# Causal softmax: dividing by the row sums before or behind the product with the values, in a two-layer decoder on one core

## The chip, the cores and the metric

One Trainium2 chip (trn2), one of its cores. The metric is device time in microseconds. Engines: TensorE (PE; its weight loads are shown apart as PEld), VectorE (DVE), ScalarE (ACT), GpSimd (POOL) and SyncE (SP), which issues the DMAs. Each engine works through its own instructions in the order in which they were written out.

## The reference

Two layers of a decoder over 512 tokens of width 1024, all in fp32. Each layer: an RMS norm and one input projection that feeds two branches, a latent attention of eight heads with a causal softmax and a state-space scan; both are normed and go through one output projection; then a cross-attention into 256 memory tokens and a gated feed-forward part. What matters here is the softmax of the eight heads, in query blocks of 128:

```python
s = (einsum(qn[lo:hi], k_nope[:hi]) + einsum(qr[lo:hi], k_rope[:hi])).astype(float32)
s = where(mask, s, -inf)
p = softmax(s, axis=-1)
outs.append(einsum('bhqk,bhkd->bqhd', p, v[:, :, :hi]))
```

## The kernel before, in words

Activations lie feature-major: partitions are features, the free dimension is the 512 tokens. An fp32 product is made of three float32r products, of a high and a low part of each operand (`mm3`, lines 213 to 219: lines 216, 217, 218). `split` (lines 232 to 245) makes the two parts: ScalarE copies the high one (line 238), VectorE or GpSimd subtracts for the low one (line 239).

The attention of a layer is `mla` (line 746). It runs over 16 units, a head `hd` and a half `I` of the queries; a unit holds query blocks 2I and 2I+1. Scores of unit u are issued ahead of the values' product of unit u-1. For each unit:

- `mla_score` (line 693) makes four products a block into PSUM (lines 707 to 710, tag "s", three banks), the rows being queries. `softmax` (line 765) takes the negated maximum on VectorE (767), the exponential with its sum on ScalarE (768), the reciprocal of the sum on VectorE (769), and scales P by it: on VectorE (773), or on ScalarE (771) where `NORM` (line 158) says "a", which is block 3 of layer 0.
- `mla_out` (line 715) transposes P by blocks of 128x128 on TensorE (728) into PSUM banks of tag "t", splits them (lines 238, 239), and multiplies with the values (736 to 738) into a bank of tag "mm". For an even head the weight has 64 columns and the result lies in partitions 0 to 63; for an odd one the weight has 128 columns, and partitions 64 to 127 are used. Behind the second unit of a head the half is copied to `a_out`: on ScalarE for even heads (742), on VectorE for odd ones (744). Two heads share one tile `a_out[pair]` of 128x512.

Tags "t" and "mm" have two banks each (line 146); "t" also serves the row norms (lines 272 to 299) and, in the state-space branch, the gate's products (line 923).

Between the units other work is placed by `PLAN` (line 165): the scan on VectorE (`s5_scan`, line 800, operations at 818 to 822 and 848 to 851), its products on TensorE (792, 877, 892), the gate (927), and the keys and values of the memory for the cross-attention (`xkv`, line 944, evacuated at 959). `OFFS` (line 176) gives each such part a priority, and the scheduler writes out each engine's order from the priorities and from its own simulation of the times (line 1203). `row` (line 272) is the kernel's existing way of laying values of tokens along the free dimension: an fp32 product of a broadcast column with the identity (277).

After the attention, `mix_out` (line 996) norms `a_out` and adds its half of the output projection to the state-space half.

Of the kernel before, what the change touches and what calls it, by code (L numbers as in the profile page):

```python
# [13 lines left out]
AF = mybir.ActivationFunctionType  # L14
ALU = mybir.AluOpType
# [119 lines left out]
class Trunk:  # L135
    def __init__(self, ctx, tc, A, out, depth=L, dbg=None):
# [8 lines left out]
    BUFS = {"raw": 3, "whi": 2, "wlo": 2, "wraw": 2, "hi": 17, "lo": 17, "ghi": 4, "glo": 4, "tmp": 5, "tmps": 3, "R": 4, "s5b": 6, "P": 4,  # L145
            "mm": 2, "f": 1, "s": 3, "t": 2, "sm": 8, "stat": 4, "sc": 3}

    # Which engine forms the low parts and the like (per layer where there are two), and PSUM tags.
    XKV_POOL = tuple(range(16))
# [7 lines left out]
    MN_POOL, MW_POOL = ((1, 3, 5, 7), (0, 2, 4)), ((), ())  # L157
    NORM = ("vvva", "vvvv")
    YT, GT = "f", "t"
    TAIL = 2  # L160
    STOP = 0

    # What runs between the attention units of a layer: (unit, part, index), and how much later than
    # its place in the order each part may run.
    PLAN = ((
# [26 lines left out]
    @contextmanager  # L192
    def later(self, off):
        """Lower the priority of what is emitted inside."""
        self.tc.cur_priority += off
        yield
        self.tc.cur_priority -= off
# [3 lines left out]

# [1 line left out]
    def load_w(self, ap, eng=None):  # L203
# [17 lines left out]
    def after(self, ins, dep):  # L221
        """Keep ins behind dep in the schedule (no wait)."""
        if dep is not None:
            self.tc.add_manual_dep(ins.ins, dep.ins.name,
                                   mybir.DependencyInfo(mybir.DependencyClass.NoSync, mybir.DependencyReason.DATA),
                                   reason="order")
        return ins
# [4 lines left out]
    def split(self, src, scale=None, out=None, lo_eng=None, dep=None):  # L232
        """src (* scale) as the exact sum of two float32r parts."""
        nc = self.nc
        eng = lo_eng or nc.vector
        hi, lo = out or self.slot()
        if scale is None:
            a = nc.scalar.activation(hi, src, AF.Copy)  # L238
            b = eng.tensor_tensor(lo, src, hi.bitcast(F32), ALU.subtract)  # L239
        else:  # L240
            a = nc.scalar.activation(hi, src, AF.Copy, scale=scale)
            b = eng.scalar_tensor_tensor(lo, src, scale, hi.bitcast(F32), ALU.mult, ALU.subtract)  # L242
        self.after(a, dep)
        self.after(b, dep)
        return hi, lo

    def load_w_slots(self, ap):
        """A narrow weight block, kept in operand slots of 512 columns."""
        out = []
        for c in range(0, ap.shape[-1], 512):  # L250
            n = min(512, ap.shape[-1] - c)
            raw = self.t([128, 512], "raw")[:, :n]
            self.nc.sync.dma_start(raw, ap[:, c:c + n])
            out.append(self.split(raw, out=[x[:, :n] for x in self.slot()]))
        return out

    def square(self, acc, x, eng=None, tag="tmp"):
        """Add the squares of x to acc."""
        sq = self.t([128, 512], tag)[:, :x.shape[-1]]
        self.nc.scalar.activation(sq, x, AF.Square)  # L260
        if acc is None:
            return sq
        (eng or self.nc.vector).tensor_tensor(acc, acc, sq, ALU.add)
        return acc
# [7 lines left out]
    def row(self, col):  # L272
        """Values of tokens down the partitions, laid along the free dimension of every partition."""
        nb = col.shape[-1]
        ps = self.p("t")[:, :nb * 128]
        for b in range(nb):
            self.nc.tensor.matmul(ps[:, b * 128:(b + 1) * 128], col[:, b:b + 1].to_broadcast([128, 128]), self.ident,
                                  start=True, stop=True)
        return ps

    def rms(self, acc, dim):
        """1/rms per token, as a column and along the free dimension."""
        nc = self.nc
        acc = acc if isinstance(acc, list) else [acc]
        n = acc[0].shape[-1]
        nb = n // 128
        ps = self.p("t")
        for b in range(nb):
            for i, x in enumerate(acc):
                nc.tensor.matmul(ps[:, b:b + 1], x[:, b * 128:(b + 1) * 128], self.ones, start=i == 0,  # L290
                                 stop=i == len(acc) - 1)
        ms = self.t([128, 4], "stat")[:, :nb]
        nc.vector.tensor_scalar(ms, ps[:, :nb], 1.0 / dim, EPS, ALU.mult, ALU.add)
        col = self.t([128, 4], "stat")[:, :nb]
        nc.gpsimd.tensor_tensor(col, ms, self.mhalf[:, :nb], ALU.pow)
        ps2 = self.row(col)
        R = self.t([128, 512], "R")[:, :n]
        nc.scalar.activation(R, ps2, AF.Copy)
        return col, R

# [1 line left out]
    def setup(self):  # L302
# [93 lines left out]

# [1 line left out]
    def load_pk(self, l):  # L398
# [165 lines left out]

# [1 line left out]
    def normed(self, l, name):  # L566
# [14 lines left out]
    def mm_block(self, ap, X, ps, m=128, eng=None):  # L581
        """One output tile [m, 512] of W^T X."""
        hi, lo = self.pre.pop(0) if self.pre else self.load_w(ap, eng)
        self.mm3(ps, [((hi[:, k * m:(k + 1) * m], lo[:, k * m:(k + 1) * m]), X[k]) for k in range(len(X))])
# [82 lines left out]
    def mla_qk(self, l, hd):  # L667
        """Key and query operands of one head: rows [nope | rope | swapped rope], or rope first for odd heads."""
        nc = self.nc
# [22 lines left out]

    def mla_score(self, qk, I):
        """Softmax rows of query blocks 2I and 2I+1."""
        nc = self.nc
# [4 lines left out]
        else:  # L700
            sc = [(self.p("s")[:, :384], self.t([128, 512], "P")[:, :384]), (self.p("s"), self.t([128, 512], "P"))]
        st = self.t([128, 8], "sm")
        for ii, (ps, p) in enumerate(sc):
# [7 lines left out]
        for ii, (ps, p) in enumerate(sc):  # L711
            self.softmax(ps, p, st[:, 4 * ii:4 * ii + 4], self.NORM[self.l][2 * I + ii])
        return [p for _, p in sc]

    def mla_out(self, hd, I, p, po):
        nc = self.nc
# [22 lines left out]
        if I == 1:  # L739
            a = a_out[pair]  # L740
            if par == 0:
                nc.scalar.activation(a[0:64], po[0:64], AF.Copy)
            else:
                nc.vector.tensor_copy(a[64:128], po[64:128])

    def mla(self, l, hooks):
# [4 lines left out]
        for u in range(2 * H + 1):  # L751
            if u < 2 * H:
                hd, I = u // 2, u % 2
                pend.append((hd, I, self.mla_score(qk[hd], I)))
            if u >= 1:
                out = pend.pop(0)
                if out[1] == 0:
                    po = self.p("mm")
                self.mla_out(*out, po)
            if u < 2 * H and I == 0 and 0 < hd < H - 1:  # L760
                qk[hd + 1] = self.mla_qk(l, hd + 1)
            for f, a in hooks.get(u, ()):
                f(*a)

    def softmax(self, ps, p, st, eng):
        nc = self.nc
        nc.vector.tensor_reduce(st[:, 0:1], ps, mybir.AxisListType.X, ALU.max, negate=True)
        nc.scalar.activation(p, ps, AF.Exp, bias=st[:, 0:1], accum_out=st[:, 1:2])
        nc.vector.reciprocal(st[:, 2:3], st[:, 1:2])
        if eng == "a":  # L770
            nc.scalar.activation(p, p, AF.Copy, scale=st[:, 2:3])
        else:
            (nc.gpsimd if eng == "p" else nc.vector).tensor_scalar(p, p, st[:, 2:3], None, ALU.mult)

# [25 lines left out]
    def s5_scan(self, l, piece):  # L800
# [9 lines left out]
        def step(dst, src, k, nj):  # L810
            """dst += A^k src (complex, over [128, 2, 16, nj])"""
            t1 = self.t([128, 2, 16, 8], "sc")[:, :, :, :nj]
# [51 lines left out]
    def s5_y0(self, q):  # L864
        """The part of y that no state carries."""
        nc = self.nc
# [77 lines left out]
    def xkv(self, l, X, ms):  # L944
        """Key (first half) and value columns of the memory, both feature-major."""
        nc = self.nc
# [31 lines left out]
    def mix_s(self, l):  # L978
        """The state-space half of the output projection's operands."""
        self.load_h(self.A["xT"] if l == 0 else self.dh)  # L980
# [3 lines left out]
    def mix_w(self, l, m, tag):  # L984
        """The state-space half of one output tile."""
        ps = self.p(tag) if tag else self.pm()
# [220 lines left out]
```

## Time and profile before

| | |
|---|---|
| median of 3 runs | 1632.43 us |
| the runs | 1628.01, 1632.43, 1634.59 us |
| span of the profiled execution | 1624.2 us (first to last instruction; its own time is not listed beside it) |
| mean granted TensorE clock | 0.966 of full |
| busy: PE, DVE, ACT, POOL | 1517.3, 975.1, 619.6, 345.8 us |

Spans are those of one profiled execution; start and end of a run lie around them. "Busy" leaves out waits, branches and DMA issues. The granted clock is the share of full speed that TensorE's throttle let through: 1.0 is 2.4 GHz, 0.5 is 1.2 GHz. Starts are counted from the span's first instruction.

### The profile page before, as it was taken

Reading aid. Unit: us, or ns where it says so; the run is one execution under the profiler, and the core shown is the slowest. Engines: PE = TensorE matmul, PEld = TensorE weight load, DVE = VectorE, ACT = ScalarE, POOL = GpSimd, SP = SyncE. Lnnn points to the kernel's source line nnn. Section 1 sums busy time; section 2 is a strip of 40 time slices with the busy share of each in tenths; the row PEclk is TensorE's granted clock in tenths of the full one; section 3 lists DMA queues with packets and bytes.
Section 4 is the critical chain, followed back from the end, with each engine's and each line's share of the span. In section 5 each row is a group of like instructions: output and inputs, shape, how many; then the busy total and the mean of one; then the engine's idle time right before and its main releaser. Section 6 shows DMA issues by size and latency. Waiting matters only on the chain.

```text
span 1624.2 us, 20486 instructions
## 1 busy us (share of the span) xinstructions
PE 1517.3 (93%) x8038; PEld 1272.5 (78%) x8038; DVE 975.1 (60%) x1499; ACT 619.6 (38%) x995; POOL 345.8 (21%) x225
## 2 busy tenths in 40 slices
PE   7779798999999999999998778989999999999997
PEld 6558687788778888888886777878888888888886
DVE  6985966866764434435453996685555443443554
ACT  5344357444333313223242534753443331322333
POOL 4553443402421100101100354430000110010110
PEclk9879799999999999999999989999999999999998
DMA  6174444321443232232248515332212222223222
GB/s 224 62 130 105 85 138 135 105 91 42 127 136 99 103 96 99 89 106 91 88 156 155 133 42 146 124 118 93 75 41 92 93 102 99 96 91 105 91 90 75
DMA packets 97488, 169.09 MB, mean 104 GB/s; under 512 B 32496, under 2 KB 55536, under 8 KB 97392
## 3 DMA queue, kind: packets, MB, share of 16 engines
q1 hardware_dynamic: 97392, 167.79, 34.7%
q8 instruction: 63, 1.03, 0.3%
q14 instruction: 33, 0.27, 0.1%
HBM read 150.00 MB, written 15.66 MB: 102 GB/s over the span
## 4 chain that ended last, share of the span: by engine, by line
PE 67%; DVE 9%; ACT 4%; DMA 2%; issue 2%; POOL 1%; SPq 1%; DVEq 0%; ACTq 0%; POOLq 0%
PE mm L216 13%; PE mm L218 13%; PE mm L217 12%; PE f L216 7%; PE f L217 7%; PE f L218 7%; ACT whi L209 1%; DVE lo L239 1%; ACT hi L238 1%; DVE s5b L927 1%; DVE wlo L210 1%; DVE sc L818 1%; PE mm L1006 1%; PE mm L1005 1%; DMA s5b<-du 1%
## 5 line engine op out<-in xcount | busy, mean ns | idle before, releaser
L209 ACT ACTIVATE whi<-wraw 128x1024 fp32r<-128x1024 f32 (+1 forms) x234 | 243.3, 1042 | 637.1 <-PE mm L217 312.3
L210 DVE TENSOR_TENSOR wlo<-wraw,whi 128x1024 fp32r<-128x1024 f32 (+2 forms) x196 | 279.4, 1426 | 68.1 <-ACT whi L209 65.9
L216 PE MATMUL mm<-hi,whi 128*128 128x512 f32 x589 | 231.3, 393 | 0.3 <-ACT whi L209 0.3
L218 PE MATMUL mm<-hi,wlo 128*128 128x512 f32 x589 | 230.0, 392 | 0.4 <-DVE wlo L210 0.4
L217 PE MATMUL mm<-lo,whi 128*128 128x512 f32 x589 | 229.7, 391 | 0.0
L1113 POOL TENSOR_TENSOR tmp<-tmp,tmp 128x512 f32<-128x512 f32 x44 | 60.4, 1374 | 573.8 <-DVE tmp L1112 518.9
L216 PE MATMUL mm<-ghi,whi 128*128 128x512 f32 (+1 forms) x368 | 147.1, 400 | 9.3 <-ACT whi L209 7.9
L218 PE MATMUL mm<-ghi,wlo 128*128 128x512 f32 (+1 forms) x368 | 146.5, 398 | 0.4 <-DVE wlo L210 0.4
L217 PE MATMUL mm<-glo,whi 128*128 128x512 f32 (+1 forms) x368 | 146.0, 398 | 0.2 <-DVE glo L239 0.2
L216 PE MATMUL f<-ghi,whi 128*128 128x256 f32 (+2 forms) x432 | 144.2, 334 | 0.0
L218 PE MATMUL f<-ghi,wlo 128*128 128x256 f32 (+2 forms) x432 | 143.0, 331 | 0.8 <-POOL wlo L210 0.8
L217 PE MATMUL f<-glo,whi 128*128 128x256 f32 (+2 forms) x432 | 142.8, 331 | 0.3 <-DVE glo L242 0.3
L216 PEld LDWEIGHTS mm<-hi,whi 128*128 128x128 f32 x589 | 110.9, 188 | 26.2 <-ACT whi L209 2.2
L218 PEld LDWEIGHTS mm<-hi,wlo 128*128 128x128 f32 x589 | 110.7, 188 | 24.5 <-DVE wlo L210 0.8
L217 PEld LDWEIGHTS mm<-lo,whi 128*128 128x128 f32 x589 | 110.8, 188 | 22.9
L210 POOL TENSOR_TENSOR wlo<-wraw,whi 128x1024 fp32r<-128x1024 f32 x38 | 92.0, 2422 | 122.0 <-ACT whi L209 97.2
L216 PE MATMUL f<-hi,whi 128*128 128x512 f32 (+1 forms) x293 | 114.6, 391 | 0.3 <-ACT whi L209 0.3
L218 PE MATMUL f<-hi,wlo 128*128 128x512 f32 (+1 forms) x293 | 114.3, 390 | 0.0
L217 PE MATMUL f<-lo,whi 128*128 128x512 f32 (+1 forms) x293 | 114.2, 390 | 0.0
L964 DVE TENSOR_TENSOR s5b<-mm,s5b 128x512 f32<-128x512 f32 x52 | 35.9, 690 | 108.2 <-PE mm L218 95.9
L238 ACT ACTIVATE hi<-tmp 128x512 fp32r<-128x512 f32 (+1 forms) x100 | 63.0, 630 | 89.4 <-POOL tmp L1113 58.9
L216 PEld LDWEIGHTS f<-ghi,whi 128*128 128x128 f32 (+1 forms) x432 | 83.0, 192 | 8.9 <-issue 0.7
(296 smaller groups left out, 2976.0 us busy)
## 6 DMA issues: line engine op xcount, KB each, us to landing
wraw<-w_gate SPq DMA_DIRECT2D x44, 512.0 KB, 3.2
wraw<-w_up SPq DMA_DIRECT2D x44, 512.0 KB, 3.3
wraw<-w_xkv SPq DMA_DIRECT2D x32, 512.0 KB, 3.5
wraw<-w_down SPq DMA_DIRECT2D x30, 448.0 KB, 3.3
wraw<-w_out SPq DMA_DIRECT2D x16, 512.0 KB, 3.4
wraw<-w_xq SPq DMA_DIRECT2D x16, 512.0 KB, 3.3
wraw<-w_xo SPq DMA_DIRECT2D x16, 512.0 KB, 3.3
wraw<-w_down SPq DMA_DIRECT2D x16, 512.0 KB, 3.2
```

The lines of the kernel that those rows point to most:

```text
L209: nc.scalar.activation(hi, raw, AF.Copy)
L210: (eng or nc.vector).tensor_tensor(lo, raw, hi.bitcast(F32), ALU.subtract)
L216: self.nc.tensor.matmul(ps, wh, xh, start=i == 0, stop=False)
L217: self.nc.tensor.matmul(ps, wh, xl, start=False, stop=False)
L218: last = self.nc.tensor.matmul(ps, wl, xh, start=False, stop=i == n - 1)
L238: a = nc.scalar.activation(hi, src, AF.Copy)
L239: b = eng.tensor_tensor(lo, src, hi.bitcast(F32), ALU.subtract)
L818: E0.tensor_tensor(t1[:, ri], src[:, ri], c(Are), ALU.mult)
L927: nc.vector.tensor_tensor(self.so[m].rearrange("p (j s) -> p s j", s=8), yS[:, m], sg.rearrange("p (s j) -> p s j", s=8), ALU.mult)
L964: self.nc.vector.tensor_tensor(self.hs[m], ps, self.hs[m], ALU.add)
L1005: self.nc.tensor.matmul(ps, hi[:, ks], xh, start=False, stop=False)
L1113: nc.gpsimd.tensor_tensor(uf, uf, gf, ALU.mult)
```

## The change

P is no longer scaled. The sums of a pair of heads are collected in one tile `sums` of [128, 2, 4] (query in the partition; head of the pair; query block), the values are multiplied by the unscaled exponentials, and the half of each head is copied to `a_out` on ScalarE, for odd heads too. Once per pair, behind the odd head's copy, one VectorE instruction takes the reciprocals of all eight columns, eight fp32 products of a broadcast column (a weight of 64 columns) with the identity lay them out as rows in a PSUM bank of tag "t" (partitions 0 to 63 for the even head, 64 to 127 for the odd one), and one VectorE instruction multiplies the pair's `a_out` by it. The diff also drops comments; apart from these it is:

```diff
-            "mm": 2, "f": 1, "s": 3, "t": 2, "sm": 8, "stat": 4, "sc": 3}
+            "mm": 2, "f": 1, "s": 3, "t": 2, "sm": 5, "sums": 3, "stat": 4, "sc": 3}
...
-    NORM = ("vvva", "vvvv")
...
-    def mla_score(self, qk, I):
+    def mla_score(self, hd, qk, I):
...
-        st = self.t([128, 8], "sm")
+        if hd % 2 == 0 and I == 0:
+            self.sums = self.t([128, 2, 4], "sums")
+        st = self.t([128, 2], "sm")
...
         for ii, (ps, p) in enumerate(sc):
-            self.softmax(ps, p, st[:, 4 * ii:4 * ii + 4], self.NORM[self.l][2 * I + ii])
-        return [p for _, p in sc]
-
-    def mla_out(self, hd, I, p, po):
+            nc.vector.tensor_reduce(st[:, ii:ii + 1], ps, mybir.AxisListType.X, ALU.max, negate=True)
+            nc.scalar.activation(p, ps, AF.Exp, bias=st[:, ii:ii + 1],
+                                 accum_out=self.sums[:, hd % 2, 2 * I + ii:2 * I + ii + 1])
+        return [p for _, p in sc], self.sums
+
+    def mla_out(self, hd, I, p, sums, po):
...
         if I == 1:
             a = a_out[pair]
-            if par == 0:
-                nc.scalar.activation(a[0:64], po[0:64], AF.Copy)
-            else:
-                nc.vector.tensor_copy(a[64:128], po[64:128])
+            rr = slice(64 * par, 64 * par + 64)
+            nc.scalar.activation(a[rr], po[rr], AF.Copy)
+            if par == 1:
+                inv = self.t([128, 2, 4], "sums")
+                nc.vector.reciprocal(inv, sums)
+                pr = self.p("t")
+                for b in range(4):
+                    for x in range(2):
+                        nc.tensor.matmul(pr[64 * x:64 * x + 64, b * 128:(b + 1) * 128],
+                                         inv[:, x, b:b + 1].to_broadcast([128, 64]), self.ident, start=True, stop=True)
+                nc.vector.tensor_tensor(a, a, pr, ALU.mult)
...
-                pend.append((hd, I, self.mla_score(qk[hd], I)))
+                pend.append((hd, I, *self.mla_score(hd, qk[hd], I)))
...
-    def softmax(self, ps, p, st, eng):
-        nc = self.nc
-        nc.vector.tensor_reduce(st[:, 0:1], ps, mybir.AxisListType.X, ALU.max, negate=True)
-        nc.scalar.activation(p, ps, AF.Exp, bias=st[:, 0:1], accum_out=st[:, 1:2])
-        nc.vector.reciprocal(st[:, 2:3], st[:, 1:2])
-        if eng == "a":
-            nc.scalar.activation(p, p, AF.Copy, scale=st[:, 2:3])
-        else:
-            (nc.gpsimd if eng == "p" else nc.vector).tensor_scalar(p, p, st[:, 2:3], None, ALU.mult)
```

## Rows read from the trace of the kernel before

**Rows 1.** The page: busy time and instructions by engine; the chain's shares.

```profile
PE 1517.3 (93%) x8038; PEld 1272.5 (78%) x8038; DVE 975.1 (60%) x1499; ACT 619.6 (38%) x995; POOL 345.8 (21%) x225
...
PE 67%; DVE 9%; ACT 4%; DMA 2%; issue 2%; POOL 1%; SPq 1%; DVEq 0%; ACTq 0%; POOLq 0%
```

**Rows 2.** Stretches: length; busy PE, PEld, DVE, ACT, POOL; clock, DMA share, GB/s.

```profile
147.60:208.10 60.50, 47.98 (x303) 44.28 (x303) 59.76 (x129) 21.91 (x48) 27.33 (x16) 0.80 0.33 66
208.10:280.00 71.90, 64.37 (x470) 58.94 (x469) 44.60 (x87) 49.03 (x91) 27.66 (x16) 1.00 0.48 147
904.60:984.30 79.70, 61.00 (x372) 54.97 (x373) 77.99 (x155) 32.22 (x63) 40.81 (x23) 0.86 0.34 81
984.30:1075.00 90.70, 85.79 (x619) 78.96 (x618) 58.80 (x113) 55.52 (x107) 35.31 (x19) 0.99 0.42 133
```

**Rows 3.** Groups of instructions: count, busy us, mean ns, idle before.

```profile
L773 DVE TENSOR_SCALAR P<-P,sm 128x128 f32<-128x128 f32 (+3 forms) x56 | 32.7, 594 | 0.5
L769 DVE RECIPROCAL sm<-sm 128x1 f32<-128x1 f32 x64 | 9.6, 154 | 13.1 <-ACT P L768 12.9
L744 DVE COPY s5b<-mm 64x512 f32<-64x512 f32 x8 | 5.6, 694 | 1.3 <-PE mm L738 1.2
L690 DVE TENSOR_TENSOR tmp<-mm,R 128x512 f32<-128x512 f32 x16 | 10.9, 681 | 5.3 <-PE mm L218 5.3
L771 ACT ACTIVATE P<-P,sm 128x512 f32<-128x512 f32 x8 | 5.8, 721 | 14.0 <-DVE sm L769 13.9
L742 ACT ACTIVATE s5b<-mm 64x512 f32<-64x512 f32 x8 | 4.7, 583 | 1.8 <-PE mm L738 1.8
```

**Rows 4.** Two of these stretches, the scalings on line 773 alone.

```profile
147.60:208.10 60.50, 2.44 (x7) 0.80 0.33 66
904.60:984.30 79.70, 10.38 (x12) 0.86 0.34 81
```

**Rows 5.** Timeline of DVE: start us, length us, instruction, idle before it.

```profile
223.69 0.15 DVE L769 RECIPROCAL sm<-sm 128x1 f32<-128x1 f32 x1
223.76 0.27 DVE L773 TENSOR_SCALAR P<-P,sm 128x128 f32<-128x128 f32 x1
...
194.72 4.02 DVE L849 TENSOR_TENSOR tmps<-nAim,Sj 128x512 f32<-128x512 f32 x2
...
978.10 1.25 DVE L773 TENSOR_SCALAR P<-P,sm 128x128 f32<-128x128 f32 x1
...
982.52 1.73 DVE L773 TENSOR_SCALAR P<-P,sm 128x256 f32<-128x256 f32 x1
987.88 1.16 DVE L239 TENSOR_TENSOR lo<-t,hi 128x384 fp32r<-128x384 f32 x2 [3.62 <-ACT hi L238]
```

**Rows 6.** Timeline of PE, with the idle time before an instruction and what ended it.

```profile
199.62 0.90 PE L728 MATMUL t<-const,P 128*128 128x128 f32 x3 [2.95 <-ACT P L771]
...
215.28 0.30 PE L728 MATMUL t<-const,P 128*128 128x128 f32 x1 [1.50 <-DVE P L773]
...
981.94 0.90 PE L728 MATMUL t<-const,P 128*128 128x128 f32 x3 [0.82 <-DVE P L773]
...
349.66 1.05 PE L277 MATMUL t<-const,stat 128*128 128x128 f32 x8
350.55 0.38 PE L1067 MATMUL t<-const,s5b 128*128 128x128 f32 x2
...
139.88 0.34 PE L792 MATMUL s<-s5b,s5b 128*64 128x64 f32 x4
140.14 0.39 PE L218 MATMUL f<-ghi,wlo 128*128 128x256 f32 x1
```

**Rows 7.** Timeline of ACT, the last exponential before 981.94.

```profile
977.58 0.47 ACT L768 ACTIVATE P<-s,sm 128x256 f32<-128x256 f32 x1
```

**Rows 8.** Two short stretches, columns as in rows 2: L792 running alone; after PE's wait.

```profile
126.00:127.00 1.00, 1.00 (x34) 1.00 (x32) 0.55 (x2) 0.03 (x1) 0.00 (x0) 0.79 0.59 57
983.04:986.46 3.42, 3.42 (x18) 3.42 (x17) 1.22 (x1) 0.00 (x0) 1.06 (x1) 0.50 0.79 190
```

## The prediction

> **What bounds the kernel now.** I read the page first [rows 1]: TensorE (PE) is busy for 93% of the span and carries 67% of the chain that ended last; VectorE (DVE) carries 9%. So a microsecond counts only where PE waits. The change touches the attention part of the two layers alone, so next I cut these parts into stretches [rows 2]. In layer 0 from 147.6 to 208.1 us DVE is busy for 59.76 of 60.50 us and PE for 47.98 at a mean clock of 0.80; in layer 1 from 904.6 to 984.3 it is DVE 77.99 of 79.70, PE 61.00 at 0.86. There DVE sets the pace: the state-space scan and the softmax share its one queue. In the two stretches behind (208.1 to 280.0 and 984.3 to 1075.0) DVE is down to 44.60 of 71.90 and 58.80 of 90.70, and PE is busy for 64.37 and 85.79 at full clock: there PE sets the pace, with 7.5 and 4.9 us idle. Then I read what the removed instructions cost [rows 3, 4], how closely DVE's short instructions follow one another [rows 5], and what PE waits for [rows 6].
>
> **What DVE loses.** Gone are 56 scalings of P (32.7 us), 64 reciprocals of one column (9.6) and eight copies of an odd head's half (5.6) [rows 3]: 47.9 us. New are eight reciprocals over [128, 2, 4] and eight multiplications of 128x512 out of PSUM. The nearest rows are the one-column reciprocal, 0.15, and L690, a 128x512 product out of PSUM, 0.68; together 0.83 a pair, 6.6 us. But busy times overlap: the scaling starts 0.07 us after the reciprocal that lasts 0.15 [rows 5]. By starts a reciprocal costs 0.07, and everything else 0.08 less than it lasts: a new pair 0.7.
>
> Layer 0, DVE's stretch: 7 scalings, 2.44 us [rows 4], less 7 x 0.08 is 1.9; ten reciprocals (seven, and three whose block was scaled on ScalarE) are 0.7; a copy 0.6. One pair ends here: 0.7 comes in. Net -2.5. Bounds: -1.7 (the stretch passes part of its gain to other waits) to -4.0 (full busy times).
>
> Layer 1, DVE's stretch: 12 scalings, 10.38 us [rows 4]. Several are stretched: 128x128 takes 0.27 us at 223.76 and 1.25 at 978.10 [rows 5]. What stretches them may stretch the instruction in their place. The last four (978.10 to 984.25, 5.5 us) I take apart. The other eight are 4.9 us; I keep an unstretched part, estimated by layer 0's 2.44 / 7 = 0.35 each: 2.8. With 12 x 0.07 for reciprocals, 0.6 for the copy, and 0.7 coming in: -3.5. The last four are a plain wait: the last exponential ends at 978.05 [rows 7], but PE gets its last transposes only at 981.94 [rows 6]. The changed transposes wait for exponentials alone, so I take 3.0 off. Late next is the low half of the transposed block: DVE's split at 987.88 waits 3.62 us for ScalarE [rows 5]. After this wait PE runs 18 products at the granted clock 0.50, from 983.04 to 986.46 [rows 8], the lower of its two levels (1.2 GHz); at 2.4 GHz they would take half, so 1.7 us come back if the wait goes. Sum: -8.2. Bounds: -3.0 (unstretched parts only, PE held by something else) to -13.9 (12.2 by busy times and the clock).
>
> **Two more waits in layer 0.** PE sat idle 2.95 us before 199.62 for a scaling on ScalarE, and 1.50 before 215.28 for one on DVE [rows 6]. The first scaling's reciprocal stood behind 4.02 us of scan on DVE [rows 5]. Both waits lose their cause, but the low half of the first block still has to pass the same DVE queue, so I take half of the first: -3.0 in all. Bounds: 0 to -4.5.
>
> **ScalarE.** Eight scalings of 0.72 go, eight copies of 0.58 come [rows 3]. Layer 0 behind 208.1 us loses four and gains three: -1.1, half of which I count (it is busy 49.03 of 71.90 us [rows 2]): -0.5. Layer 1 only gains copies, three of them behind 984.3; they cost nothing while ScalarE is busy for 55.52 of 90.70 us, and 1.7 if that cover is gone. The copy can start only after the head's last product, and the next exponentials stand behind it.
>
> **What PE gains.** A pair adds eight fp32 products of 128 columns against a 64-column weight, alternating between the halves of the array. The row for full-width weights: eight issues (two a product) take 0.89 us, 349.66 to 350.55 [rows 6], so 16 would take 1.78. The row for half weights in alternating halves (L792, 64 columns): 34 issues in 1.00 us at a mean clock of 0.79 [rows 8], 0.029 each, so the halves run side by side; 128 columns are twice that, 0.059, 16 issues 0.94. Entering and leaving costs too: four such issues take 0.26 us until the next product, 139.88 to 140.14 [rows 6], 0.14 more than 4 x 0.029; I allow 0.25 for both ends. So 1.2 a pair, between 0.9 and 2.03. I am nearest to L792, whose weights have this shape. In each layer the first pair falls into DVE's stretch, where PE has idle time; the other six fall where PE sets the pace: 7.2 us, half of it in the 12.4 us of idle: +3.6. Bounds: 0 to 16.2 (eight uncovered at 2.03).
>
> The Trainium skill says otherwise of the price: "FP8 and Floating Point Precision", TensorE Precision Notes, has true fp32 as four passes through the array. At 2.4 GHz that is an estimated 0.213 us for each 128-column product, 1.95 a pair with the ends, +5.9 in place of +3.6, and a time of 1624.1. Full width agrees (0.89 / 4 = 0.222); the halves, with 0.058 for 64 columns where the rule gives 0.107, do not, so I stay with the row.
>
> **At nothing.** The maxima, exponentials and sums stay; a new shape of the sums' tile adds no instruction. No DMA is moved or added, so SP's queue and GpSimd stay as they are. The last pair's division lies at the end of each layer's attention (copy 0.58, then multiplication 0.68, for a copy of 0.69); the state-space half of the output projection covers it, or it costs 0.6 a layer.
>
> **Sum.** -2.5 - 8.2 - 3.0 - 0.5 + 3.6 = -10.6 us. The profiled execution has a span of 1624.2; its own time is not listed beside it, and the median of the three runs, 1632.43, lies 8.2 above that span. I apply the change to both: span 1613.6, time 1621.8. The bounds sum to -24 (1608) and +14 (1646).
>
> **The rivals.** (1) The products do not overlap and find no idle time: six pairs x 2.03 = 12.2 in place of 3.6, so 1630.4, no change. For it: full-width issues cost 0.111 each. Against: L792.
> (2) The bank: slower. The row of reciprocals takes one of only two "t" banks until the multiplication, which waits for the copy and stands in DVE's order behind scan or gating work. The transposes of the next heads need that bank, and PE, which issues in order, stops with everything behind. One scan multiplication is 2.0 us (4.02 for two [rows 5]); with 1.0 lost to the lower clock afterwards, eight pairs x 3.0 = 24, so 1646. It decides from (10.6 + 8.2) / 8 = 2.4 us a pair. Against: a pair comes once in four units of attention, and layer 0's two stretches (132 us [rows 2]) hold most of its 16 units, so some 8 us each.
> (3) More than forecast: DVE's freed time also moves the scan and PSUM evacuations ahead, and all upper bounds hold: 1608.
> (4) The transposes still wait just as long, for the exponentials or for the low halves: then layer 1 gives 3.5 of its 8.2 and the two waits 0, so 1621.8 + 7.7 = 1629.5, no change. I count it within (1).
>
> **How the numbers follow.** A measurement of this kernel can tell about 0.5%, 8.2 us, from no change. Forecast 0.45 (gains of 5 to 16 us: 0.28 faster, 0.17 same); (1) with (4) 0.18, same; (3) 0.15, faster; (2) 0.22, slower. Faster 0.43, same 0.35, slower 0.22. The range runs from (3), 1608, to 1641, which takes in (1) and most of (2) at up to 2.4 us a pair; the rest of (2) is what I leave out.
>
> **What would show it.** Right: DVE busy about 41 us less in all; L728 waiting for exponentials or for nothing; 128 new half-width issues at about 0.06 us; PE's clock near 1.0 behind the last units of DVE's stretch in layer 1; mean busy time of the new multiplication near 0.68. Wrong: the new products at 0.11; transposes or other "t" users waiting for the new multiplication (rival 2); DVE's stretches as long as before though it does less; or PE waiting as long for the low halves as it did for the scaling.

## The result, and the profile after

The changed kernel is slower: a median of 1642.40 us (1640.71 to 1647.96, 4 runs) against 1632.29 (1628.01 to 1634.59, 4 runs) for the kernel before; ratio 1.0078, 95% interval 1.0054 to 1.0102. The forecast was 1621.8, 10.6 us faster. The two profiled executions lie further apart than the medians, 1646.2 against 1624.2 us of span: the one after is the slowest of its runs, the one before, with some 1.8 us around its span, lies 6 us under its median. So below, times between two places of one profile are compared where they can be, and totals by medians.

The page after, busy time and the chain's shares, answering to [rows 1]:

```profile
PE 1541.3 (94%) x8166; PEld 1293.7 (79%) x8166; DVE 946.2 (57%) x1387; ACT 620.3 (38%) x995; POOL 346.9 (21%) x225
...
PE 73%; DVE 12%; ACT 5%; DMA 4%; issue 2%; POOL 1%; SPq 1%; DVEq 0%; ACTq 0%; POOLq 0%
```

VectorE does less, as announced (28.9 us less instead of some 41, because the instructions that stayed got longer on balance), but TensorE carries more of the chain. The stretches of [rows 2] in the profile after; layer 1 starts 11.7 us later there (`in_proj`, line 597 before and 596 after: 869.23 instead of 857.49), so its two stretches are moved by that:

```profile
147.60:208.10 60.50, 53.46 (x345) 49.09 (x346) 56.61 (x113) 25.24 (x54) 27.16 (x15) 0.83 0.35 72
208.10:280.00 71.90, 63.86 (x431) 56.63 (x430) 35.08 (x57) 43.36 (x83) 24.47 (x15) 0.92 0.45 126
916.30:996.00 79.70, 64.19 (x396) 57.83 (x396) 72.97 (x137) 34.92 (x68) 38.83 (x24) 0.83 0.37 78
996.00:1086.70 90.70, 82.77 (x588) 75.25 (x586) 44.83 (x69) 53.21 (x103) 33.38 (x18) 0.96 0.41 126
```

In the first and third stretch TensorE does more than before (345 and 396 matmuls for 303 and 372): the freed VectorE lets it go ahead. In the second and fourth it does less (431 for 470, 588 for 619), and its granted clock falls from 1.00 and 0.99 to 0.92 and 0.96. What was won in front is lost behind. The new groups of instructions:

```profile
L752 PE MATMUL t<-const,sums 128*64 128x128 f32 x128 | 12.2, 307 | 0.0
...
L745 ACT ACTIVATE s5b<-mm 64x512 f32<-64x512 f32 x16 | 9.4, 588 | 8.2 <-PE mm L741 8.1
...
L754 DVE TENSOR_TENSOR s5b<-s5b,t 128x512 f32<-128x512 f32 x8 | 5.5, 686 | 16.5 <-ACT s5b L745 13.5 <-PE t L752 2.7 <-ACT P L714 0.3
```

The multiplication costs what was said (0.686 for 0.68), but VectorE stands idle for 16.5 us in front of its eight, 13.5 of them until ScalarE has copied the odd half.

**Where the time is lost.** Two places in each layer can be read in every profile: the last transposes of P, and the first transposes of the cross attention behind the output projection. Before (x80 and x16: the last number of the first and third row, and the first start of the second and fourth):

```profile
L728 PE MATMUL t<-const,P x80: 270/273/476, 114.7 to 271.6; 128*128 128x128 f32 x80
...
L1067 PE MATMUL t<-const,s5b x16: 270/272/273, 350.6 to 391.7; 128*128 128x128 f32 x16
...
L728 PE MATMUL t<-const,P x80: 270/273/474, 938.8 to 1064.1; 128*128 128x128 f32 x80
...
L1067 PE MATMUL t<-const,s5b x16: 270/272/273, 1141.9 to 1184.0; 128*128 128x128 f32 x16
```

After:

```profile
L731 PE MATMUL t<-const,P x80: 270/273/421, 113.9 to 278.0; 128*128 128x128 f32 x80
...
L1067 PE MATMUL t<-const,s5b x16: 270/272/273, 362.4 to 403.6; 128*128 128x128 f32 x16
...
L731 PE MATMUL t<-const,P x80: 270/273/329, 947.8 to 1082.6; 128*128 128x128 f32 x80
...
L1067 PE MATMUL t<-const,s5b x16: 271/272/273, 1163.9 to 1206.1; 128*128 128x128 f32 x16
```

From the one place to the other, "the end" from here on, it took 79.0 and 77.8 us before and takes 84.4 and 81.3 after: 5.4 and 3.5 us, at the place where the forecast had put the division "at nothing". Another 6.4 us of layer 0 lie in front of its last transposes, and 6.7 between layer 0's cross attention and layer 1's last transposes (720.2 us instead of 713.5); with the one profile the longest and the other near the shortest of its runs, these two are upper bounds.

### The profile page after: what moved, and what is told of

The parts are those of the page before. It is cut to its first block, busy times and chain, and to the rows that moved or that the text cites. A ratio compares the mean times of both kernels' runs of the same rounds, so it can differ in the third digit from the quotient of the medians.

```text
span 1646.2 us, 20665 instructions
## 1 busy us (share of the span) xinstructions
PE 1541.3 (94%) x8166; PEld 1293.7 (79%) x8166; DVE 946.2 (57%) x1387; ACT 620.3 (38%) x995; POOL 346.9 (21%) x225
## 4 chain that ended last, share of the span: by engine, by line
PE 73%; DVE 12%; ACT 5%; DMA 4%; issue 2%; POOL 1%; SPq 1%; DVEq 0%; ACTq 0%; POOLq 0%
PE mm L215 13%; PE mm L217 13%; PE mm L216 13%; PE f L215 7%; PE f L217 7%; PE f L216 7%; DMA s5b<-dQ 1%; ACT whi L208 1%; ACT hi L237 1%; DVE sc L818 1%; DVE lo L238 1%; DMA s5b<-du 1%; PE t L276 1%; PE s L792 1%; DVE s5b L974 1%
```

## The experiments

The ratio of each run is to the kernel before on the same chip (its medians there were 1630.90 to 1633.24 us); ends in layer 0 / layer 1 as just defined, each from one profile. e12 to e15 follow in the text. The scheduler lays out the queues of every run anew, so a difference of 2 or 3 us between two runs can also come from other orders.

| run | median us (lowest to highest) | ratio to before (95%) | ends us |
|---|---|---|---|
| e1 no division | 1629.44 (1625.35 to 1635.14) | 0.9983 (0.9966 to 1.0000) | 79.6 / 78.5 |
| e2 odd half by VectorE | 1642.02 (1638.90 to 1644.10) | 1.0053 (1.0028 to 1.0077) | 84.9 / 81.4 |
| e3 two units later | 1644.00 (1641.50 to 1649.15) | 1.0080 (1.0053 to 1.0107) | 84.8 / 82.4 |
| e4 before, odd half by ScalarE | 1636.03 (1631.35 to 1643.26) | 1.0029 (1.0007 to 1.0050) | 79.5 / 78.8 |
| e5 last row in an s buffer | 1633.82 (1630.63 to 1636.84) | 1.0017 (1.0002 to 1.0032) | 78.5 / 78.6 |
| e6 last pair scaled | 1634.52 (1631.80 to 1641.11) | 1.0030 (1.0015 to 1.0046) | 79.6 / 78.9 |
| e8 last pair alone divided | 1638.25 (1634.71 to 1639.87) | 1.0040 (1.0023 to 1.0057) | 85.1 / 80.8 |
| e7 row early | 1654.13 (1648.70 to 1657.76) | 1.0140 (1.0110 to 1.0171) | 79.2 / 77.8 |
| e9 load first | 1639.73 (1637.79 to 1643.00) | 1.0048 (1.0032 to 1.0063) | 84.4 / 81.2 |
| e10 = e9 + e5 | 1632.14 (1630.26 to 1635.91) | 1.0003 (0.9990 to 1.0016) | 78.5 / 79.5 |
| e11 all rows behind the scores | 1630.05 (1626.12 to 1632.55) | 0.9979 (0.9967 to 0.9992) | 78.5 / 78.7 |
| e16 = e1 + e9 | 1620.71 (1618.49 to 1624.98) | 0.9928 (0.9904 to 0.9951) | 79.5 / 79.1 |
| e18 = e11, products twice | 1636.91 (1632.76 to 1643.77) | 1.0035 (1.0018 to 1.0052) | 83.9 / 78.4 |
| e17 = e11, rows by DMA | 1647.24 (1645.98 to 1653.26) | 1.0107 (1.0080 to 1.0134) | 80.6 / 78.2 |

**First round: is it the wait in VectorE's queue?** Theory Q took the 16.5 us at their word. e1 leaves out the division, e2 takes ScalarE's copy out of the wait, e3 defers three divisions of four, e4 makes one part of the change alone.

```diff
e2
-            nc.scalar.activation(a[rr], po[rr], AF.Copy)
+            if par == 0:
+                nc.scalar.activation(a[rr], po[rr], AF.Copy)
+            else:
+                nc.vector.tensor_copy(a[rr], po[rr])
e3
+            if self.due and (u % 4 == 2 or u == 2 * H):
+                self.divide(*self.due.pop(0))
```

> The changed kernel without the reciprocal, the small products and the multiplication: its output is the undivided one. Theory Q (VectorE's queue stands behind the multiplication, 16.5 us of idle time in front of it, and the second layer part and the transposes behind it are late): all of the loss and the gain that was forecast come out, 1618 to 1624 us. Theory B (the price is the products on TensorE and the bank they hold): the same here, 1618 to 1626; the next two runs tell Q and B apart. Theory O (the order that the scheduler lays out for all engines came out worse once the scalings were gone, with the loads and GELUs of the state-space part in worse places, whatever the division costs): 1634 to 1644 us, with the loss still between 214 and 286 us and after 1010 us.

> The changed kernel with the odd head's half copied out of PSUM by VectorE, as in the kernel before, so that the multiplication waits for ScalarE no longer at its end. Theory Q: of the 16.5 us of idle time in front of the multiplications the 13.5 for ScalarE go, and the median falls by 6 to 13 us, to 1629 to 1636. Theory B: no change, 1640 to 1644 (the products and the bank stay). Theory O: no rule, anywhere between 1634 and 1646, by the order that comes out.

> The changed kernel with reciprocal, products and multiplication of the first three pairs of heads written two attention units later, by when the copies are long done; those of the last pair stay. Theory Q: the waits in front of three of four multiplications go in each layer, 1628 to 1636 us. Theory B: no change, 1640 to 1644. Theory O: no rule, 1634 to 1646.

> The kernel before with one part of the change alone: the odd head's half is copied out of PSUM by ScalarE. Theory Q: nothing waits on VectorE for it, so within 3 us of the kernel before, 1629 to 1636. If ScalarE's longer queue is itself the cause (theory A: eight copies of 0.59 us behind GELUs and splits), it is slower by 5 us or more, 1637 to 1645. Theory O: within 5 us either way.

Q fell: without ScalarE's copy in the wait (e2) or with three divisions two units later (e3) nothing came back. The odd copy on ScalarE alone (e4) costs the kernel before 4.0 us, at the edge of its range, but undone in the changed kernel (e2) it gives nothing. And e1 is a puzzle of its own: with no division at all only 2.6 us are gained, where the scalings' removal had been put at 14.2. What e1, e4 and the kernel before share, and after, e2 and e3 do not, is the short end.

**Second round: the end.** Theory N is read from TensorE's timeline at the end of layer 0. Before: the last transposes, the sums for the state-space half's norm (line 290), and the row of that norm (277).

```profile
271.40 0.52 PE L728 MATMUL t<-const,P 128*128 128x128 f32 x3
...
275.60 0.95 PE L290 MATMUL t<-ones,tmp 128*128 128x1 f32 x8
...
280.17 1.05 PE L277 MATMUL t<-const,stat 128*128 128x128 f32 x8
```

After (289 and 276 are the same two lines, 752 is the new row of reciprocals):

```profile
277.74 0.52 PE L731 MATMUL t<-const,P 128*128 128x128 f32 x3
...
283.15 1.09 PE L752 MATMUL t<-const,sums 128*64 128x128 f32 x16
...
284.80 0.78 PE L289 MATMUL t<-ones,tmp 128*128 128x1 f32 x6
...
288.64 0.28 PE L289 MATMUL t<-ones,tmp 128*128 128x1 f32 x2
...
291.50 0.38 PE L276 MATMUL t<-const,stat 128*128 128x128 f32 x2
```

All of these write to "t", which has two buffers. The new row takes one place in their order, in front of the norm of the state-space half: that norm starts 7.1 us behind the last transposes instead of 4.2, its row 13.8 instead of 8.8. But this norm is the work that was to cover the division. TensorE does not stand idle for it: it is busy from 280.6 to 293.4 us, and the last two issues of the norm's sums, at 288.64, stand behind products of the cross-attention's keys and values. So the norm is late by its place in the order that the scheduler laid out with the new row in it, not by a wait that the profile shows.

```diff
e5
-                pr = self.p("t")
+                pr = self.p("s" if pair == H // 2 - 1 else "t")
```

e6 scales P in the last pair (heads 6 and 7) as the kernel before does, e8 in the first three pairs; e7 makes the row early:

```diff
e7, in mla_score, behind the exponentials of the odd head
+        if hd % 2 == 1 and I == 1:
...
+            self.R_row = self.t([128, 512], "tmp")
+            nc.scalar.activation(self.R_row, pr, AF.Copy)
e7, in mla_out, in place of the odd head's copy
+                nc.gpsimd.tensor_tensor(a[0:64], a[0:64], R[0:64], ALU.mult)
+                nc.vector.tensor_tensor(a[rr], po[rr], R[rr], ALU.mult)
```

> The changed kernel with the last pair's row of reciprocals in one of the three PSUM buffers of the scores, which nobody uses any more by then; everything else as changed. Theory N (most of the loss lies at the end of each attention part: the row takes one of the two t buffers in front of the norm of the state-space half, so that the norm, which should cover the division, starts after it): the time from the last transposes to the cross attention falls back from 84.4 and 81.3 us to 79 to 81 and 78 to 79, and the median falls by 5 to 8 us, to 1634 to 1638. Theory C (the loss comes in the course of the attention, from products and orders): 1640 to 1644, those two times unchanged.

> The changed kernel with the last pair of heads (6 and 7) scaling P as the kernel before does, and the first three pairs divided afterwards. Theory N: the end of each attention part is that of the kernel before (79.0 and 77.8 us), and the median falls by about 9 us, to 1631 to 1636. Theory C: three quarters of the loss stay, 1637 to 1643.

> The mirror of the run before: the first three pairs scale P as the kernel before does, and the last pair alone is divided afterwards. Theory N: the end costs 5.4 and 3.5 us more, so the median is 1632 + 9 = 1641, between 1637 and 1643. Theory C: 1631 to 1636.

> The changed kernel with the row of reciprocals laid out right behind the odd head's last exponentials and copied by ScalarE to the scratch memory; the odd half then leaves PSUM through the multiplication on VectorE, the even half is multiplied on GpSimd. Theory N: no t buffer is held in front of the norm and nothing is left to wait for at the end, so the ends are 79 and 78 us, and the whole comes near the kernel without a division, 1629 to 1634. Theory C: the products and 8 more copies of 0.59 us on ScalarE stay in the course, 1637 to 1645.

N holds, from both sides. One word, another PSUM tag for the last row, brings 8.6 us, a little more than expected, and the two ends get shorter by as much (5.9 and 2.7); e6 gives nearly the same (7.9), and its mirror e8 has the long ends and loses 6.2 against the kernel before. In e5 the norm is back in its place, 4.2 and 8.8 us behind the last transposes:

```profile
279.67 0.52 PE L731 MATMUL t<-const,P 128*128 128x128 f32 x3
...
283.86 0.95 PE L289 MATMUL t<-ones,tmp 128*128 128x1 f32 x8
...
288.43 1.05 PE L276 MATMUL t<-const,stat 128*128 128x128 f32 x8
```

The Trainium skill, "Perfetto Trace Analysis", Matmuls, wants independent groups of matmuls to rotate through different PSUM banks; e5 gives one group a bank outside "t", and the trace agrees so far as the norm behind it starts 4.2 us behind the last transposes and not 7.1. e7 missed: its ends are short, but the last transposes of layer 0 come at 287.0, 15 us behind the kernel before; there ScalarE waits for the products (6.4 us in layer 0) with the splits behind it, and TensorE 9.0 us for low halves. Which of its parts does it was not tried.

**Third round: the order of the loads.** In the profile after, the chain in front of the last transposes of layer 0 runs through SP's queue, where before it did not. That queue before (`dCA` holds a matrix for the scan's output, y is that output, `dy` its copy in memory):

```profile
228.71 0.32 SPq L891 DMA_DIRECT2D raw<-dCA  x1
229.51 6.09 SPq L903 DMA_DIRECT2D s5b<-dy  x8
235.90 0.34 SPq L899 DMA_DIRECT2D dy<-s5b  x1
```

After:

```profile
229.83 5.19 SPq L903 DMA_DIRECT2D s5b<-dy  x8
235.12 0.54 SPq L891 DMA_DIRECT2D raw<-dCA  x1
245.29 0.33 SPq L899 DMA_DIRECT2D dy<-s5b  x1
```

The scheduler, which laid out all queues anew, put the last load of `dCA` behind the eight transfers of the first half of y. The second half then leaves 9.4 us later. In layer 1 the load stands in front of them in both. VectorE's queue has its part in it: in the profile after, the multiplication of the third pair waits 6.83 us, and the addition that ends y (line 895) stands behind it:

```profile
240.72 0.69 DVE L754 TENSOR_TENSOR s5b<-s5b,t 128x512 f32<-128x512 f32 x1 [6.83 <-ACT s5b L745]
...
244.58 0.67 DVE L895 TENSOR_TENSOR s5b<-s5b,f 128x512 f32<-128x512 f32 x1
```

e9 puts that load first again, by emitting the eight transfers behind it; e10 adds e5; e11 defers three divisions until the last scores are issued, with all rows in "s".

```diff
e9, in s5_y
+        if q == 3:
+            self.y_out(0, load)
e11, in mla
+            while u == 2 * H and self.due:
+                self.divide(*self.due.pop(0))
             if u >= 1:
                 out = pend.pop(0)
```

> The changed kernel with one order put right on SP's queue: the last load of dCA stands ahead of the eight transfers of the first half of y, as it does in the kernel before (the changed schedule has it behind them). Theory S (the loss in the course of layer 0's attention, 6.4 us up to its last transposes, is the second half of y that leaves 9.4 us later, at 245.29 instead of 235.90, because of this load and of the multiplication ahead of its addition on VectorE): the second transfer of y starts 4 to 8 us earlier and the median falls by 2 to 6 us, to 1636 to 1640; the ends stay at 84 and 81 us. Without this effect: 1641 to 1645.

> The order of the run before and the last row in a buffer of the scores together. If the two causes add up (N 8.6 us, S 2 to 6 us): 1628 to 1632, at or below the kernel before. If S is nothing: 1632 to 1636.

> The run before, and the first three pairs are divided only behind the last scores too, all rows in buffers of the scores, so that no division stands in VectorE's queue or in a t buffer in the course. Theory Q+S: nothing of the division is left in the course, the whole comes to the kernel without a division (1629.4) or to 3 us below it: 1626 to 1631. If the twelve products and multiplications pile up at the end instead: 1633 to 1640.

The medians of e9 and e11 came as written, and e10's lies 0.14 us above its range. The second half of y leaves at 236.04 in e9, 9.3 us earlier and not the 4 to 8 announced, and the last transposes of layer 0 come 4.4 us earlier; the 2.7 us of e9's median are at the edge of what the two ratios separate (1.0048 and 1.0078). With both causes mended, e10 is level with the kernel before, e11 0.2% faster. e11 beats both kernels, the changed one by 12 us and the one before by 2.6.

**Fourth round: where did the forecast gain go?** First suspicion, theory G: GpSimd's half of the scan's last step, which stands behind VectorE's freed time.

```diff
e12 (e11 with it), e13 (the kernel before with it), e14 and e15 (e11, layer 0 or 1 alone)
-            for ri, (c2, E) in enumerate(((nAim, V), (Aim, P))):
+            for ri, (c2, E) in enumerate(((nAim, V), (Aim, V))):
```

> The run before (all rows behind the scores, load first) with GpSimd's half of the scan's last step moved to VectorE, which the change has given time. Theory G (the time that VectorE gains in front of the scan's end is lost behind it: without a division the scan of layer 0 ends 3.3 us earlier, at 190.91 instead of 194.25, but the last of its results leaves at 212.64 instead of 212.76, because GpSimd's part stands there between splits of weights and queries): the last transfer of the scan's results starts 4 us earlier or more in each layer and the median falls by 2 to 7 us, to 1623 to 1628. Theory P (TensorE's own work sets the end of these parts, whatever comes earlier): 1628.5 to 1632.

> The same move in the kernel before, as a control: there VectorE is busy for 59.76 of 60.50 us in front of this place and still has the scalings to do. Theory G: no gain or a loss, 1630 to 1640, so that the move pays only together with the change. If it gains as much here, it has nothing to do with the change.

> The run with the join on VectorE, in layer 0 alone (layer 1's half stays on GpSimd). Both layers together had executions from 1621.78 to 1639.09 us, and the profiled one, at 1624.81, was 4 us ahead in layer 0. Theory G in layer 0: the cross attention of layer 0 starts about 4 us earlier than at 349.5 and the median is 1624 to 1628, with a spread as of e11 (6 us). Theory P: 1628.5 to 1632. If layer 0 is where the executions differ: a spread of 15 us or more here.

> The same in layer 1 alone. Theory G gives little here, as the profiled execution gained under 1 us in layer 1: 1628 to 1631. If layer 1 is where the executions differ: a spread of 15 us or more, with a median of 1633 to 1638.

e12: 1635.75 (1621.78 to 1639.09, ratio 0.9990 to 1.0042); e14: 1629.99 (1625.54 to 1634.91, 0.9970 to 1.0001); e15: 1632.24 (1624.88 to 1634.24, 0.9953 to 0.9999). None is clearly better than e11's 1630.05, so G is not what holds the gain back; why e12's executions spread over 17 us stays open. The control, e13, is 1652.12 (1650.79 to 1657.33; 1.0110 to 1.0162): 21 us more for the same move where VectorE still has the scalings. That is in line with the first step of the forecast: before the change VectorE had no time to spare there.

> The kernel without any division (its output is the undivided one) with the last load of dCA ahead of the eight transfers as well: all that the change takes off VectorE, none of what it adds, and the order of the kernel before. Theory P (TensorE and its clock set the end of these parts, so that VectorE's freed time is worth little): 1625 to 1629, a gain of 3 to 7 us against the kernel before. If the forecast gain of 13.7 us was held back by that order alone: 1617 to 1621.

This missed its theory P and met the other reading: 1620.71, 11.9 us faster than the kernel before. In e1 the one misplaced load hid 8.7 us of the gain: the second half of y leaves at 231.54 in e16 and at 240.21 in e1, and the last transposes of layer 0 come at 266.7 and 273.3. So between e16 and e11 a division costs 9.3 us, and the last two runs ask whether that is the products' price on TensorE.

```diff
e18, in divide
-        for b in range(4):
+        for b in range(4) if last else [0, 1, 2, 3] * 2:
e17, in mla_out
+                    nc.sync.dma_start(sums_d.rearrange("x b q -> q x b"), sums)
```

> As the run with all rows behind the scores, but the rows of the first three pairs of each layer are laid out by DMA (reciprocals to DRAM in row order, read back onto 64 partitions each), so that 96 of the 128 small products leave TensorE. Theory P (TensorE sets the pace of these parts, and the products cost their full 1.2 us a pair, 9.3 us in all between 1620.71 without a division and 1630.05 with it): 6 x 1.2 = 7 us less, 1622 to 1626. If the 9.3 us are something else (multiplications on VectorE, the last pair's end, orders): 1628 to 1633.

> As the run with all rows behind the scores, but each product of the first three pairs of each layer is issued twice, 96 more of 16 issues a pair. Theory P: 6 x 1.0 to 1.2 = 6 to 7 us more, 1635.5 to 1638. If the products hide in idle time: 1629 to 1632.

The median of e18 came as theory P wrote, 6.9 us more than e11's (9.1 by the ratios), which for 48 products more, 96 issues, would be 1.14 us for each of six pairs. But the profile puts most of it elsewhere. The late rows of layer 1 lie between the same two transposes in e16 (none), e11 (64 issues) and e18 (112); the stretch, with TensorE's busy time first:

```profile
1032.23:1050.24 18.01, 18.01 (x111) 16.09 (x110) 7.22 (x8) 9.65 (x15) 7.18 (x3) 1.00 0.51 175
1037.64:1060.08 22.44, 22.44 (x175) 19.50 (x174) 9.30 (x12) 9.66 (x15) 7.19 (x3) 1.00 0.42 141
1041.27:1066.50 25.23, 25.23 (x229) 22.80 (x227) 10.73 (x14) 10.56 (x19) 7.16 (x3) 1.00 0.34 116
```

TensorE has no idle time in any of the three and the full clock, so each product shows: 64 issues more take 4.4 us, 1.1 a pair, and 54 more (48 of them of the doubled products) another 2.8. In layer 0 the same count, again e16, e11, e18:

```profile
236.52:266.36 29.84, 24.05 (x140) 20.71 (x139) 13.30 (x16) 21.86 (x35) 9.48 (x4) 0.94 0.32 102
240.89:270.78 29.89, 28.87 (x195) 23.01 (x193) 15.00 (x19) 20.48 (x32) 9.52 (x4) 0.95 0.31 97
240.48:272.45 31.97, 31.97 (x243) 24.43 (x241) 15.30 (x19) 20.74 (x33) 9.53 (x4) 1.00 0.30 93
```

There e16 has 5.8 us of idle time, the rows of e11 fit into it and cost nothing, and only the doubled ones of e18 show, with 2.1 us. So 4.4 of the 9.3 us between e16 and e11 are the products of layer 1; 4.3 lie in layer 0 in front of these rows (its transposes run at 240.89 instead of 236.52), and what costs them stays open. And e18's number is in part luck. Its profile is 6.3 us longer than e11's, and 5.4 of them lie at the end of layer 0, behind the doubled products. There the row of the state-space half's norm comes 11.8 us behind the last transposes instead of 8.8: GpSimd's step in that norm (line 294) starts 4.2 us behind VectorE's (277.30), because the low part of a weight was laid out in front of it, where in e11 it starts 0.2 us behind (275.95). The rest of the 5.4 was not traced. In e18:

```profile
279.10 2.39 POOL L209 TENSOR_TENSOR wlo<-wraw,whi 128x1024 fp32r<-128x1024 f32 x1 [2.38 <-ACT whi L208]
281.45 1.46 POOL L294 TENSOR_TENSOR stat<-stat,mhalf 128x4 f32<-128x4 f32 x1
```

and in e11:

```profile
276.19 1.02 POOL L294 TENSOR_TENSOR stat<-stat,mhalf 128x4 f32<-128x4 f32 x1 [0.84 <-DVE stat L292]
```

In layer 1 the 2.8 us do not reach the end: from the cross attention of layer 0 to the last transposes of layer 1 e18 and e11 both take 717.2 us. e17 could not answer: its transfers of the reciprocals wait 17.5 us for VectorE at the head of SP's queue in layer 0, with the scan's transfers behind them.

## Why the prediction was wrong, step by step

**What VectorE loses, and the two waits** (-2.5 - 8.2 - 3.0, with -0.5 on ScalarE: -14.2). Right in the sum: with the order of the kernel before, taking the scalings off gives 11.9 us (e16 against its own runs of before), and e13 is in line with the reading behind it. How the 11.9 divide among the terms is not shown: the profile of before, 6 us under its median, is only 4.7 us longer than that of e16, and 4.9 us of difference lie in front of layer 0's last transposes alone.

**What TensorE gains** (+3.6). The price of a pair was right, the cover was right in one layer of e11 and wrong in the other. The trace has 16 issues in 1.09 us (283.15 above), against 0.94 and 0.25 for both ends in the forecast. "Half of it in the 12.4 us of idle" failed in layer 1, where e11 pays 4.4 us for four pairs, all of it; in layer 0 the rows of e11 found idle time. In the changed kernel, where the rows stand elsewhere, their price was not measured apart. Rival (1) had half of this right: that no idle time is found, not that the products do not overlap. The Trainium skill's price, "FP8 and Floating Point Precision", TensorE Precision Notes, four passes for true fp32, an estimated 1.95 a pair, does not agree with these rows either: the products with weights of 64 columns in alternating halves ran at 0.06 to 0.07 us an issue.

**At nothing: the last pair's division.** This is the step that cost most; with it mended alone (e5) the change is within 0.2% of the kernel before. "The state-space half of the output projection covers it, or it costs 0.6 a layer": it costs 8.6 us in all (e5 against the changed kernel), because the row of the division takes a place among the "t" buffers in front of its own cover. Rival (2) named the right resource, the "t" buffers, and the wrong victim: the transposes do not wait for the multiplication (no wait of TensorE is ended by the multiplication), but the norm behind them comes late. That norm does not wait for the multiplication either: in layer 0 it starts at 284.80, the multiplication at 285.62. The rival said "The transposes of the next heads need that bank" and never asked who uses it when there is no next head.

**At nothing: "no DMA is moved".** Failed. The program moves none, but its instructions' order is laid out by a scheduler, and in the new layout one load of layer 0 stands behind eight transfers. Putting it back brings 2.7 us here (e9), 8.7 us in the kernel without a division (e16 against e1).

**VectorE's queue.** The forecast let the multiplication wait for the copy only within rival (2). Three of four divisions moved out of the course bring 2.1 us (e10 against e11, which also moves their rows out of "t"), not the 13.5 of idle time in front of the multiplications.

The chain of runs from the kernel before to the changed one, through e16, e11, e10 and e9, reads -11.9 + 9.3 + 2.1 + 7.6 + 2.7 = +9.8 us; the medians of the changed kernel say +10.1, the ratio +12.7. That the chain comes out is no proof, since each step is the difference of two neighbours. The parts depend on one another: the tag brings 8.6 us alone and 7.6 behind the mended load, the load 2.7 or 8.7. What is shown by itself is the tag's part and, by e16 against e1, the load's; of the 9.3 us, 4.4 are placed.

Of the signs named for the forecast: TensorE's idle time in front of the transposes, for P, fell from 8.0 to 1.5 us in both layers together, and those 1.5 are for exponentials; the issues took 0.06 to 0.07 us, the multiplication 0.686; the clock behind VectorE's stretch of layer 1 is 1.00 from 990 to 1022 us: all right. VectorE lost 29 us and not 41, and over the whole of the two stretches behind the clock fell (0.92 and 0.96). Of the signs against it, "other 't' users waiting" comes nearest: another user of "t" is late, though it waits for its place and not for the multiplication.

## What to carry to other kernels

Before a step is called covered, list the buffers that it takes and see whether its cover needs them: a PSUM tag with two buffers is a queue, and the place of one new tile in it can cost more than the tile's own work. Where a scheduler lays out the queues, a change anywhere can move a load; compare the orders of the queues before looking for deeper reasons, and pin the loads that a chain hangs on. Idle time in front of an instruction is not its cost: here 16.5 us of it were worth about 2. And a run that lands in its range can do so for another reason, as e18 does: look where in the profile its microseconds lie.

## What the runs showed of the hardware

Turning 1,024 reciprocals into row order by DMA, in pieces of 4 bytes, took longer than 512 KB of weights. From issue to landing in e17, least, median and most:

```profile
DMA to landing us min/median/max: 9.0/11.8/12.3
```

and the weights in the profile after (median):

```profile
wraw<-w_gate SPq DMA_DIRECT2D x44, 512.0 KB, 3.3
```

The Trainium skill, "Perfetto Trace Analysis", DMA Optimizations, warns of the cost of a transfer below 2 KB; the trace agrees, with 4 KB in 4-byte pieces at 3.6 times the time of 512 KB. And executions of one kernel differ together with TensorE's clock: of the 120 executions of the kernel before that were measured beside e1 to e18, the 11 with a mean granted clock of 0.958 or less have a median of 1636.16 us, the 24 with 0.965 or more one of 1628.98. Which of the two brings the other with it is not shown.
